# Two one-hots from table products, weight splits one block ahead, and a larger early share of gather steps in a PEER encoder kernel

## The chip, the core and the metric

The kernel runs on one core of a Trainium2 chip. The metric is the time of one execution on the device, in microseconds (us). The core has a matrix engine (TensorE, PE in the rows, with its weight loads as PEld), a vector engine (VectorE, DVE), a scalar engine (ScalarE, ACT), GpSimd (POOL) and a sync engine (SyncE, SP). Each engine runs its own instructions strictly in the order in which they stand in its queue. Sixteen DMA engines move data between the device's memory, where all inputs and the kernel's DRAM buffers lie, and the on-chip memory (SBUF). TensorE writes into PSUM.

## The reference

One encoder layer on 1024 tokens of width 1024. The change lies in its last part, the PEER feed-forward: each token picks, for each of 8 heads, 16 of 16384 experts; an expert number is e = 128 i + j.

```python
def chunk(xc):
    q = (xc @ w_q).reshape(C, PEER_HEADS, 2, PEER_DK // 2)
    s = jnp.einsum('chpd,hpnd->chpn', q, sub_keys, preferred_element_type=jnp.float32)
    sv, si = lax.top_k(s, PEER_TOPK)
    ...
    best, pos = lax.top_k(cand, PEER_TOPK)
    eidx = jnp.take_along_axis(cidx, pos, axis=-1)
    g = jax.nn.softmax(best, axis=-1)
    u = u_tab[eidx]
    a = jax.nn.gelu(jnp.einsum('chkd,cd->chk', u, xc, ...), approximate=False)
    vv = v_tab[eidx]
    return jnp.einsum('chk,chkd->cd', (g * a).astype(vv.dtype), vv)
```

## The kernel before

The 1024 tokens are 8 tiles of 128. Tiles 0 to 2 are **gathered**: for each of a token's 128 chosen experts one indirect DMA on GpSimd brings that expert's row of 1024 values for each of the tile's 128 tokens (tile `grow`, 128x1024, six buffers), first rows of the u table, which VectorE multiplies with the token (L1249), then rows of the v table, which it adds to `gacc` (L1257). One such row load with its use is called a gather use here; there are 3 x 256 = 768. Tiles 3 to 7 (640 tokens) are **dense**: all 16384 experts are computed for them, as 128 blocks of 128 experts.

A dense **u block** (`u_part`) loads 512 KB of transposed weights into `ur` (one buffer), splits them into a high and a low part (`uh` by a ScalarE copy, L291; `ul` by a VectorE subtraction, L292; two buffers each), does 2 x 8 x 3 matmuls of 320 columns (L285 to L287, three for each product of split numbers) into PSUM, and a GELU into `A`. Blocks 1 to 72 (EARLY) run in the early stage, use the four PSUM buffers `ps_x`, and store `A` to DRAM (`a_d`); the other 56 run in the late stage. I number the blocks by the order of their `ul` on VectorE: "split 10" is the L292 of the tenth.

The late stage weighs each block's `A` with a dense gate matrix G (L1359) and multiplies the result with the v table (`vr`, `vh`, `vl`; 128 blocks in two halves of 512 columns, 15 matmuls each).

G is built in the early stage. `route` finds the chosen experts of a tile on VectorE (some 180 instructions a tile). For a dense tile it writes j, and j*j in two parts, to DRAM (`jx_d`) and reads it back as `jl`, and transposes i and the gates into `ig`. `build_g` then goes through the tile in 32 **hot steps** of four tokens: the one-hot of i (`p1`) is an is_equal on VectorE (L1160); the one-hot of j times the gate (`p2`) comes from a product of `jl` with the table `par_r` (L1153, "parabola": 2*j*j' - j*j - j'*j' + 1, which is 1 where j = j' and not positive elsewhere) and a Relu on ScalarE (L1166); four matmuls of `p2` and `p1` give four tokens' G (L1182), ScalarE copies them out (L1183), and every eighth step 2 MB go to `g_d`.

The order is not written out by hand. The program order is set by generators: before each early block so much of `weights()` (routing and hot steps) as its planned cost asks for, after it so many gather steps as `tick` pays for. EHEAD is the share of the gather steps that the early stage is planned to do. A scheduler then orders each engine's queue by its own estimate of times; a buffer of a pool is handed on in program order.

Of the kernel before, what the change touches and what calls it, by code (L numbers as in the profile page):

```python
# [282 lines left out]
def mm3(nc, out, L, R, start, stop):  # L283

    nc.tensor.matmul(out, L[0], R[0], start=start, stop=False)  # L285
    nc.tensor.matmul(out, L[0], R[1], start=False, stop=False)  # L286
    nc.tensor.matmul(out, L[1], R[0], start=False, stop=stop)  # L287


def split(nc, hi, lo, src):  # L290
    nc.scalar.copy(hi, src)  # L291
    return nc.vector.tensor_sub(lo, src, hi)  # L292
# [3 lines left out]
def layer(ctx: ExitStack, tc: tile.TileContext, a: dict, out: bass.AP):  # L296
    nc = tc.nc
# [9 lines left out]
    dram = ctx.enter_context(tc.tile_pool(name="dram", bufs=1, space=DRAM))  # L307
    ident = const.tile([P, P], F32, name="ident")
# [237 lines left out]
    with tc.tile_pool(name="rqp", bufs=1, side="right") as rqp:  # L546
# [4 lines left out]
        for cts, ones in (((0, 1), ones_q), ((2,), ones_kv)):  # L551
# [6 lines left out]
            r = rqp.tile([P, T], F32, name="r")  # L558
# [7 lines left out]
    for j in (*range(4, 12), *range(4)):  # L566
# [166 lines left out]
    with tc.tile_pool(name="ltp", bufs=2, side="right") as ltp:  # L733
# [70 lines left out]
        for c in range(2):  # L804
            cs = slice(256 * c, 256 * c + 256)
# [119 lines left out]
    iota = keep.tile([P, P], F32, name="iota")  # L925
# [89 lines left out]
    def route(tt, rp, done):  # L1015
# [69 lines left out]
        ij = rp.tile([P, 2, P], I32, name="r_ij")
        nc.vector.tensor_scalar(ij[:, 0], ei, 7, None, op0=ALU.arith_shift_right)
        nc.vector.tensor_scalar(ij[:, 1], ei, 127, None, op0=ALU.bitwise_and)
        ijf = rp.tile([P, P], F32, name="r_ijf")
        nc.vector.tensor_copy(ijf, ij[:, 0])
        jj = rp.tile([P, P], I32, name="r_jj")  # L1090
        nc.vector.tensor_tensor(jj, ij[:, 1], ij[:, 1], op=ALU.mult)
        jp = rp.tile([P, 2, P], I32, name="r_jp")
        nc.vector.tensor_scalar(jp[:, 1], jj, 127, None, op0=ALU.bitwise_and)
        nc.vector.tensor_scalar(jp[:, 0], jj, 127 << 7, None, op0=ALU.bitwise_and)
        jx = rp.tile([P, 3, P], BF16, name="r_jx")
        nc.vector.tensor_copy(jx[:, 0], ij[:, 1])
        nc.vector.tensor_copy(jx[:, 1:3], jp)
        nc.sync.dma_start(jx_d[tt].rearrange("r t s -> t r s"), jx)
        jl = jls[tt % 2]
        for r in range(3):  # L1100
            nc.sync.dma_start(jl[32 * r:32 * r + 32], jx_d[tt, r].rearrange("(q t) s -> t q s", t=32))
        ps = psO.tile([P, 2, P], F32, name="ps_o0")
        nc.tensor.transpose(ps[:, 0], ijf, ident)
        nc.tensor.transpose(ps[:, 1], w.rearrange("p h k -> p (h k)"), ident)
        ig = rp.tile([P, 2, P], F32, name="ig", bufs=2)
# [28 lines left out]
    CS = 32  # L1134
    GI = 4
    NCS = TD // CS
    jx_d = dram.tile([NT, 3, P, P], BF16, name="jx_d")
    NB = 4
    HOT = 0.69
    g_d = dram.tile([NCS, P, P, CS], F32, name="g_d")  # L1140
# [1 line left out]
    def build_g(ijg, t, gp):  # L1142


        ig, jl = ijg
        steps = [(cs, c4) for cs in range(P // CS) for c4 in range(0, CS, NB)]
        par, hot = {}, {}

        def parabola(n):
            cs, c4 = steps[n]  # L1150
            ps = psO.tile([P, NB, P], F32, name=f"ps_o{n % 2}")
            c = cs * CS + c4
            nc.tensor.matmul(ps, jl[0:98, c // 32], par_r[0:98, c % 32:c % 32 + NB], start=True, stop=True)  # L1153
            par[n] = ps

        def hots(n):
            cs, c4 = steps[n]
            c = cs * CS + c4
            p1 = gp.tile([P, NB, P], F32, name="p1", bufs=4)
            nc.vector.tensor_tensor(p1, iota.unsqueeze(1).to_broadcast([P, NB, P]),  # L1160
                                    ig[:, 0, c:c + NB].unsqueeze(2).to_broadcast([P, NB, P]),
                                    op=ALU.is_equal)
            p2 = gp.tile([P, NB, P], F32, name="p2", bufs=4)
            ps = par.pop(n)
            for j in range(NB):
                nc.scalar.activation(p2[:, j], ps[:, j], AF.Relu, scale=ig[:, 1, c + j:c + j + 1])  # L1166
            hot[n] = p1, p2

        parabola(0)
        parabola(1)  # L1170
        hots(0)
        for n, (cs, c4) in enumerate(steps):
            if n + 2 < len(steps):
                parabola(n + 2)
            if n + 1 < len(steps):
                hots(n + 1)
            if c4 == 0:
                st = gp.tile([P, P, CS], F32, name="gst", bufs=2)
            p1, p2 = hot.pop(n)
            ps = psH.tile([P, NB, P], F32, name="ps_h")  # L1180
            for j in range(NB):
                nc.tensor.matmul(ps[:, j], p2[:, j], p1[:, j], start=True, stop=True)  # L1182
            nc.scalar.copy(st[:, :, c4:c4 + NB], ps.rearrange("p c i -> p i c"))  # L1183
            if c4 + NB == CS:
                nc.sync.dma_start(g_d[t * (P // CS) + cs], st)
            yield HOT


# [103 lines left out]
    with tc.tile_pool(name="rp", bufs=1, side="left") as rp, \  # L1292
# [249 lines left out]
```

## Time and profile before

| | us |
|---|---|
| median of 3 runs (3285.90 to 3292.27) | 3290.01 |
| the profiled execution | 3294.61 |
| its span on the core | 3292.8 |
| the early stage: from split 3 to split 74 | 1077.9 to 1925.1 |
| the late stage, from split 74 to the end of the span | 1925.1 to 3292.8 |

The profiled execution is 1.8 us longer than its span and 4.6 us above the median of the runs. Over the whole span PE is busy 91%, VectorE 83%, ScalarE 38% and GpSimd 32%; PE's granted clock is 0.959 of full speed (2.4 GHz) in the mean. Stages differ, so everything below is read by stage.

### The profile page before, as it was taken

The page shows a single profiled execution, that of the slowest core. Times are in us where ns is not written, and L with a number is a line of the kernel's source. Part 1 is how long each engine was busy: PE and PEld are TensorE (multiplying, and loading weights), DVE is VectorE, ACT ScalarE, POOL GpSimd, SP SyncE. Part 2 cuts the span into 40 slices and gives each one's busy share as a digit, 9 for nine tenths or more (in the row PEclk, how much of TensorE's full clock was granted, in tenths as well). Part 3 has the DMA queues.
Part 4 walks back from the last instruction along what each step waited for, and adds up shares of the span by engine and source line. Part 5 has one row for each costly group of instructions (what it writes and reads, how often), then busy time and mean ns, then how long its engine had stood idle before and what let it go on. Part 6 is the DMA issues. An engine that isn't in the chain of part 4 may idle for free.

```text
span 3292.8 us, 44912 instructions
## 1 busy us (share of the span) xinstructions
PE 3005.8 (91%) x15582; PEld 2558.8 (78%) x15582; DVE 2734.7 (83%) x5514; ACT 1256.6 (38%) x2454; POOL 1052.8 (32%) x797
## 2 busy tenths in 40 slices
PE   6999788889999779999898789998999999899997
PEld 5676566556699679888897778886888888788886
DVE  7556788888757899999998758888888888888877
ACT  4544434455523226756564122222222222222222
POOL 0000000000000351332344726554655555555550
PEclk9999898889999889999999999999999999999999
DMA  5344733412444777877888989999999898999983
GB/s 170 104 147 141 241 106 106 109 55 64 144 154 144 280 262 239 309 273 275 309 297 314 368 299 354 332 348 352 339 341 343 312 343 310 349 329 333 333 307 134
DMA packets 355065, 828.88 MB, mean 252 GB/s; under 512 B 34345, under 2 KB 144851, under 8 KB 351253
## 3 DMA queue, kind: packets, MB, share of 16 engines
q1 hardware_dynamic: 243957, 422.25, 38.2%
q0 software_dynamic: 110592, 402.70, 34.0%
q8 instruction: 123, 2.02, 0.3%
q10 hardware_dynamic: 288, 1.05, 0.1%
q14 instruction: 105, 0.86, 0.1%
HBM read 715.52 MB, written 110.33 MB: 251 GB/s over the span
## 4 chain that ended last, share of the span: by engine, by line
PE 48%; DVE 28%; DMA 12%; issue 6%; ACT 3%; POOL 1%; SPq 1%; DVEq 0%; ACTq 0%; POOLq 0%
PE ps_x L285 8%; PE ps_x L287 8%; PE ps_x L286 8%; DMA vr<-in_peer_v 6%; DVE gacc L1257 4%; DVE grow L1249 3%; PE ps_h L287 3%; PE ps_h L285 3%; PE ps_h L286 3%; PE ps_o L286 2%; PE ps_o L285 2%; PE ps_o L287 2%; DVE ul L292 2%; DVE p L1160 2%; DMA ur<-in_peer_uT 1%
## 5 line engine op out<-in xcount | busy, mean ns | idle before, releaser
L1236 POOL DMA_INDIRECT grow<-in_peer_u,eid x384 | 532.8, 1387 | 590.2 <-DVE grow L1249 204.7
L1236 POOL DMA_INDIRECT grow<-in_peer_v,eid x384 | 506.1, 1318 | 589.7 <-DVE gacc L1257 296.1
L1257 DVE SCALAR_TENSOR_TENSOR gacc<-grow,dot,gacc 128x1024 f32<-128x1024 f32 x381 | 487.2, 1279 | 14.7 <-DMA grow<-in_peer_v,eid 10.1
L1249 DVE SCALAR_TENSOR_TENSOR grow<-grow,gh 128x1024 f32<-128x1024 f32 x384 | 459.6, 1218 | 23.5 <-DMA grow<-in_peer_u,eid 23.0
L287 PE MATMUL ps_x<-hd,ul 128*128 128x320 f32 x1152 | 370.9, 331 | 62.5 <-DVE ul L292 62.3
L285 PE MATMUL ps_x<-hd,uh 128*128 128x320 f32 x1152 | 376.8, 328 | 33.1 <-ACT uh L291 33.1
L286 PE MATMUL ps_x<-hd,uh 128*128 128x320 f32 x1152 | 372.5, 324 | 0.0
L286 PE MATMUL ps_x<-vl,wh 128*128 128x512 f32 x864 | 343.7, 398 | 4.0 <-DVE vl L292 4.0
L287 PE MATMUL ps_x<-vh,wl 128*128 128x512 f32 x864 | 338.6, 395 | 0.0
L285 PE MATMUL ps_x<-vh,wh 128*128 128x512 f32 x864 | 304.6, 400 | 31.9 <-ACT vh L291 22.2
L291 ACT CAST vh<-vr 128x512 fp32r<-128x512 f32 x256 | 155.9, 619 | 449.5 <-DMA vr<-in_peer_v 303.3
L287 PEld LDWEIGHTS ps_x<-hd,ul 128*128 128x128 f32 x1152 | 226.3, 199 | 76.6 <-DVE ul L292 73.2
L285 PE MATMUL ps_h<-hd,uh 128*128 128x320 f32 x896 | 277.7, 310 | 2.6 <-ACT A L1209 2.6
L286 PE MATMUL ps_h<-hd,uh 128*128 128x320 f32 x896 | 277.2, 310 | 0.0
L287 PE MATMUL ps_h<-hd,ul 128*128 128x320 f32 x896 | 275.4, 310 | 0.0
L292 DVE TENSOR_TENSOR vl<-vr,vh 128x512 fp32r<-128x512 f32 x256 | 173.3, 685 | 118.2 <-ACT vh L291 117.3
L285 PEld LDWEIGHTS ps_x<-hd,uh 128*128 128x128 f32 x1152 | 229.3, 199 | 40.0 <-ACT uh L291 39.0
L286 PEld LDWEIGHTS ps_x<-hd,uh 128*128 128x128 f32 x1152 | 228.8, 199 | 0.8
L285 PEld LDWEIGHTS ps_x<-vh,wh 128*128 128x128 f32 x864 | 164.3, 192 | 69.6 <-ACT vh L291 24.4
L291 ACT CAST uh<-ur 128x1024 fp32r<-128x1024 f32 x128 | 134.7, 1052 | 211.1 <-DMA ur<-in_peer_uT 121.3
L292 DVE TENSOR_TENSOR ul<-ur,uh 128x1024 fp32r<-128x1024 f32 x128 | 155.8, 1217 | 60.9 <-ACT uh L291 59.1
L286 PEld LDWEIGHTS ps_x<-vl,wh 128*128 128x128 f32 x864 | 165.8, 192 | 40.9 <-DVE vl L292 7.8
(365 smaller groups left out, 6868.3 us busy)
## 6 DMA issues: line engine op xcount, KB each, us to landing
ur<-in_peer_uT SPq DMA_DIRECT2D x128, 512.0 KB
vr<-in_peer_v SPq DMA_DIRECT2D x256, 256.0 KB
g_d<-gst SPq DMA_DIRECT2D x20, 2048.0 KB
gt<-g_d SPq DMA_DIRECT2D x32, 1280.0 KB
a_d<-A SPq DMA_DIRECT2D x72, 320.0 KB
A<-a_d SPq DMA_DIRECT2D x72, 320.0 KB
fw<-in_dft_fw SPq DMA_DIRECT2D x64, 256.0 KB
wr<-in_w_in SPq DMA_DIRECT2D x16, 512.0 KB
```

The costliest lines, as they stand in the source:

```text
L285: nc.tensor.matmul(out, L[0], R[0], start=start, stop=False)
L286: nc.tensor.matmul(out, L[0], R[1], start=False, stop=False)
L287: nc.tensor.matmul(out, L[1], R[0], start=False, stop=stop)
L291: nc.scalar.copy(hi, src)
L292: return nc.vector.tensor_sub(lo, src, hi)
L1160: nc.vector.tensor_tensor(p1, iota.unsqueeze(1).to_broadcast([P, NB, P]), ig[:, 0, c:c + NB].unsqueeze(2).to_broadcast([P, NB, P]), op=ALU ...
L1236: nc_i = nc.gpsimd.indirect_dma_start(out=t, out_offset=None, in_=a["peer_" + kind], in_offset=bass.IndirectOffsetOnAxis(ap=eid[g][:, k:k ...
L1249: nc.vector.scalar_tensor_tensor(t, t, 1.0, h_t, op0=ALU.mult, op1=ALU.mult, accum_out=d[:, k - k0:k - k0 + 1])
L1257: nc.vector.scalar_tensor_tensor(acc, t, dots[k0][:, k - k0:k - k0 + 1], acc, op0=ALU.mult, op1=ALU.add)
```

## The change

- The one-hot of i is no longer a VectorE comparison. A second table product (into a `ps_x` buffer) and a Relu of 512 columns on ScalarE make it. For this `route` writes i and j and their squares' parts as six rows (`x_d`), `jl` is loaded in six pieces, and only the gates are transposed.
- The first two steps' products of each dense tile are ordered on PE behind the last matmul of the u block written just before them (`issue_after`).
- `u_part` splits the weights of its own block and of the next one before its matmuls.
- EHEAD goes from 0.28 to 0.36.
- The stores of `A` (`a_d`) and of G (`g_d`) are issued from ScalarE's queue and no longer from SyncE's.

```diff
-EHEAD = 0.28
+EHEAD = 0.36
...
-        nc.sync.dma_start(jx_d[tt].rearrange("r t s -> t r s"), jx)
+        xx = rp.tile([P, 3, 2, P], I32, name="r_xx")
+        nc.vector.tensor_scalar(xx[:, 0, 0], ei, 7, None, op0=ALU.arith_shift_right)
+        nc.vector.tensor_scalar(xx[:, 0, 1], ei, 127, None, op0=ALU.bitwise_and)
+        x2 = rp.tile([P, 2, P], I32, name="r_x2")
+        nc.vector.tensor_tensor(x2, xx[:, 0], xx[:, 0], op=ALU.mult)
+        nc.vector.tensor_scalar(xx[:, 1], x2, 127 << 7, None, op0=ALU.bitwise_and)
+        nc.vector.tensor_scalar(xx[:, 2], x2, 127, None, op0=ALU.bitwise_and)
+        xb = rp.tile([P, 6, P], BF16, name="r_xb")
+        nc.vector.tensor_copy(xb, xx.rearrange("p r w s -> p (r w) s"))
+        nc.sync.dma_start(x_d[tt].rearrange("r t s -> t r s"), xb)
...
-            ps = psO.tile([P, NB, P], F32, name=f"ps_o{n % 2}")
             c = cs * CS + c4
-            nc.tensor.matmul(ps, jl[0:98, c // 32], par_r[0:98, c % 32:c % 32 + NB], start=True, stop=True)
-            par[n] = ps
+            par[n] = []
+            for w in range(2):
+                ps = psO.tile([P, NB, P], F32, name=f"ps_o{n % 2}") if w else psX.tile([P, NB, P], F32, name="ps_x")
+                nc.tensor.matmul(ps, jl[0:98, w, c // 32], par_r[0:98, c % 32:c % 32 + NB], start=True, stop=True)
+                par[n].append(ps)
...
-            nc.vector.tensor_tensor(p1, iota.unsqueeze(1).to_broadcast([P, NB, P]),
-                                    ig[:, 0, c:c + NB].unsqueeze(2).to_broadcast([P, NB, P]),
-                                    op=ALU.is_equal)
+            pi, pj = par.pop(n)
+            nc.scalar.activation(p1, pi, AF.Relu)
...
-        parabola(0)
-        parabola(1)
+        with tc.issue_after(ended[-1]) if ended else ExitStack():
+            parabola(0)
+            parabola(1)
...
-                nc.sync.dma_start(g_d[t * (P // CS) + cs], st)
+                nc.scalar.dma_start(g_d[t * (P // CS) + cs], st)
...
+    def u_part(i, psum):
+
+        for n in (i, i + 1):
+            if n < P and n not in ready:
+                u_load(n)
+        uh, ul = ready.pop(i)
...
-            nc.sync.dma_start(a_d[e], A)
+            nc.scalar.dma_start(a_d[e], A)
```

How the queues change, at three places. First PE, before, near block 15, where the transposes of the first dense tile's routing stand (`r_ijf`, `r_w`) and block 15 goes on around them (`ps_x_9939` is its second half; the first products stand behind block 15, inside block 16):

```order
L287 MATMUL ps_x_9939<-hd_7120,ul_9909 128x320
L1103 MATMUL ps_o0_9022<-ident_60,r_ijf_9008 128x128 [waits DVE_49]
L1104 MATMUL ps_o0_9022<-ident_60,r_w_8996 128x128
L285 MATMUL ps_x_9939<-hd_7120,uh_9908 128x320
L286 MATMUL ps_x_9939<-hd_7120,uh_9908 128x320
L287 MATMUL ps_x_9939<-hd_7120,ul_9909 128x320
```

The same place after: the transpose and the first three products of the first dense tile, which need `jl` (loaded after that tile's routing), stand directly behind block 7 (`ul_8873`) and ahead of block 8 (`ps_x_9108`):

```order
L287 MATMUL ps_x_8981<-hd_7120,ul_8873 128x320
L1100 MATMUL ps_o0_9045<-ident_60,r_w_9020 128x128 [waits DVE_49]
L1151 LDWEIGHTS jl1_7577 [waits DMAHW4_49,DMAHW6_49,DMAHW2_49,Pool_49]
L1151 MATMUL ps_x_9049<-par_r_7574,jl1_7577 128x512
L1151 LDWEIGHTS jl1_7577
L1151 MATMUL ps_x_9053<-par_r_7574,jl1_7577 128x512 [waits Activation_49]
L1151 LDWEIGHTS jl1_7577
L1151 MATMUL ps_x_9064<-par_r_7574,jl1_7577 128x512 [waits Activation_49]
L285 MATMUL ps_x_9108<-hd_7120,uh_8950 128x320 [waits Activation_49]
```

Before, blocks 8 to 15 stood ahead of the first product; after, only blocks 1 to 7 do, and block 8 stands behind it. The products take `ps_x` buffers, which the blocks use too.

Second VectorE, before, behind split 44: routing, one-hots of i and gather uses are mixed (the first 12 of the 22 rows up to split 45):

```order
L292 TENSOR_TENSOR ul_13744<-ur_13741,uh_13743 128x1024
L1027 MAX_INDEX r_si_14912<-r_sv_14911,r_s_14909 128x8
L1043 TENSOR_TENSOR r_cand_15412<-r_sv_14911 128x8
L1160 TENSOR_TENSOR p1_13828<-iota_6486,ig_13125 128x512
L1249 SCALAR_TENSOR_TENSOR grow_13804,dot_13809<-grow_13804,gh_8442 128x1024
L1257 SCALAR_TENSOR_TENSOR gacc_8444<-grow_13594,dot_12473,gacc_8444 128x1024
L1026 MAX r_sv_14911<-r_s_14909 128x8
L1249 SCALAR_TENSOR_TENSOR grow_13807,dot_13809<-grow_13807,gh_8442 128x1024
L1160 TENSOR_TENSOR p1_13928<-iota_6486,ig_13125 128x512
L1026 MAX r_sv_14911<-r_s_14909 128x8
L1160 TENSOR_TENSOR p1_13944<-iota_6486,ig_13125 128x512
L1160 TENSOR_TENSOR p1_14005<-iota_6486,ig_13125 128x512
```

VectorE after, from split 44 to split 45 complete: nothing but gather uses (L1266 is the old L1257):

```order
L292 TENSOR_TENSOR ul_13963<-ur_13960,uh_13962 128x1024
L1266 SCALAR_TENSOR_TENSOR gacc_8450<-grow_15564,dot_15038,gacc_8450 128x1024
L1266 SCALAR_TENSOR_TENSOR gacc_8450<-grow_15567,dot_15038,gacc_8450 128x1024
L1266 SCALAR_TENSOR_TENSOR gacc_8450<-grow_15662,dot_15038,gacc_8450 128x1024
L1266 SCALAR_TENSOR_TENSOR gacc_8450<-grow_15667,dot_15038,gacc_8450 128x1024
L1266 SCALAR_TENSOR_TENSOR gacc_8450<-grow_15670,dot_15038,gacc_8450 128x1024
L1266 SCALAR_TENSOR_TENSOR gacc_8450<-grow_15673,dot_15038,gacc_8450 128x1024
L292 TENSOR_TENSOR ul_14065<-ur_14062,uh_14064 128x1024
```

The one-hots are gone from VectorE and gather uses have moved forward into their place: ahead of split 74 stand 256 of the 768 uses before and 381 after.

Counted in VectorE's queue (the number of instructions that stand ahead of a split):

| ahead of | gather uses | routing | splits | one-hots of i |
|---|---|---|---|---|
| split 18, before | 53 | 527 | 17 | 6 |
| split 10, after | 56 | 547 | 9 | 0 |
| split 34, after | 154 | 1125 | 33 | 0 |
| split 74, before | 256 | 1266 | 73 | 160 |
| split 74, after | 381 | 1256 | 73 | 0 |

In the late stage the uses stand about as close as before, 28 to 42 for every 16 of the 256 splits of v weights, up to about the 180th of them; behind that no use is left after the change, where some 130 were left before. In PE's queue after, of the 160 hot steps 5 stand ahead of block 10, 69 between blocks 10 and 34, 86 between 34 and 74.

## Rows read from the trace of the kernel before

**Rows 1.** The page, part 1: busy time, share of the span, instructions.
```profile
PE 3005.8 (91%) x15582; PEld 2558.8 (78%) x15582; DVE 2734.7 (83%) x5514; ACT 1256.6 (38%) x2454; POOL 1052.8 (32%) x797
```

**Rows 2.** Windows: stretch, length, busy PE, PEld, DVE, ACT, POOL, granted clock, DMA share, GB/s.
```profile
1258.00:1500.00 242.00, 229.28 (x1608) 219.25 (x1607) 238.34 (x691) 158.20 (x441) 74.73 (x60) 0.97 0.80 288
1500.00:1754.00 254.00, 236.51 (x1658) 224.69 (x1658) 252.42 (x748) 162.26 (x447) 87.35 (x68) 0.99 0.83 295
1785.00:1890.00 105.00, 77.80 (x440) 73.08 (x438) 81.22 (x99) 16.95 (x30) 74.82 (x54) 0.87 0.95 356
1990.00:2890.00 900.00, 861.76 (x4321) 746.19 (x4320) 783.54 (x1057) 231.00 (x381) 493.09 (x364) 0.98 0.96 339
```

**Rows 3.** Groups of VectorE from 1258 to 1754: busy, mean ns; idle before.
```profile
L1160 DVE TENSOR_TENSOR p<-iota,ig 128x512 f32<-128x512 f32 x150 | 99.2, 677 | 0.9 <-PE ps_h L1182 0.9
L1257 DVE SCALAR_TENSOR_TENSOR gacc<-grow,dot,gacc 128x1024 f32<-128x1024 f32 x65 | 82.7, 1272 | 0.0
L1249 DVE SCALAR_TENSOR_TENSOR grow<-grow,gh 128x1024 f32<-128x1024 f32 x64 | 76.7, 1209 | 0.4 <-DMA grow<-in_peer_u,eid 0.4
```

**Rows 4.** Timeline of VectorE (start, length): splits 18, 58, 73, 74; four one-hots.
```profile
1234.60 2.49 DVE L1160 TENSOR_TENSOR p<-iota,ig 128x512 f32<-128x512 f32 x4
1258.04 1.23 DVE L292 TENSOR_TENSOR ul<-ur,uh 128x1024 fp32r<-128x1024 f32 x1
1754.26 1.23 DVE L292 TENSOR_TENSOR ul<-ur,uh 128x1024 fp32r<-128x1024 f32 x1 [0.39 <-ACT uh L291]
1919.05 1.23 DVE L292 TENSOR_TENSOR ul<-ur,uh 128x1024 fp32r<-128x1024 f32 x1 [4.62 <-ACT uh L291]
1925.13 1.23 DVE L292 TENSOR_TENSOR ul<-ur,uh 128x1024 fp32r<-128x1024 f32 x1 [4.86 <-ACT uh L291]
```

**Rows 5.** Timeline of VectorE in the dense stretch: two splits, gather uses between.
```profile
1859.97 1.22 DVE L292 TENSOR_TENSOR ul<-ur,uh 128x1024 fp32r<-128x1024 f32 x1
1861.11 1.22 DVE L1249 SCALAR_TENSOR_TENSOR grow<-grow,gh 128x1024 f32<-128x1024 f32 x1
...
1867.47 1.22 DVE L1249 SCALAR_TENSOR_TENSOR grow<-grow,gh 128x1024 f32<-128x1024 f32 x1 [1.79 <-DMA grow<-in_peer_u,eid]
...
1872.07 1.22 DVE L292 TENSOR_TENSOR ul<-ur,uh 128x1024 fp32r<-128x1024 f32 x1
```

**Rows 6.** Timeline of ScalarE and PE: block 7's last GELU; the first two table products.
```profile
1145.79 0.44 ACT L1209 ACTIVATE A<-ps_x 128x320 f32<-128x320 f32 x1 [1.46 <-PE ps_x L287]
...
1244.10 0.61 PE L1153 MATMUL ps_o<-par_r,jl 98*128 98x512 bf16 x2
```

**Rows 7.** Timeline of PE: neighbouring matmuls of 320 and 512 columns; four one-hot matmuls.
```profile
2403.37 0.31 PE L285 MATMUL ps_h<-hd,uh 128*128 128x320 f32 x1
2403.52 0.31 PE L286 MATMUL ps_h<-hd,uh 128*128 128x320 f32 x1
...
2406.53 0.39 PE L285 MATMUL ps_x<-vh,wh 128*128 128x512 f32 x1
2406.76 0.39 PE L286 MATMUL ps_x<-vl,wh 128*128 128x512 f32 x1
...
1257.44 1.05 PE L1182 MATMUL ps_h<-p,p 128*128 128x128 f32 x8
```

**Rows 8.** DMA issues from 1785 to 1890: count, KB each (512 KB an indirect one).
```profile
ur<-in_peer_uT SPq DMA_DIRECT2D x9, 512.0 KB
grow<-in_peer_u,eid POOLq DMA_INDIRECT x27
grow<-in_peer_v,eid POOLq DMA_INDIRECT x27
```

**Rows 9.** Timeline of ScalarE: one hot step's four Relus, and its copy out.
```profile
1257.20 1.14 ACT L1166 ACTIVATE p<-ps_o,ig 128x128 f32<-128x128 f32 x4 [0.24 <-PE ps_o L1153]
1258.53 0.59 ACT L1183 COPY gst<-ps_h 128x512 f32<-128x512 f32 x1 [0.19 <-PE ps_h L1182]
```

**Rows 10.** Timeline of VectorE in the late stage: the 94th block is weighed.
```profile
2887.59 0.82 DVE L1359 TENSOR_TENSOR A<-A,gt 128x640 f32<-128x640 f32 x1 [3.40 <-DMA gt<-g_d]
```

More of the change, by code (lines that the diff above doesn't have):

```diff
@@ L286, in mm3 @@
     nc.tensor.matmul(out, L[0], R[1], start=False, stop=False)
-    nc.tensor.matmul(out, L[1], R[0], start=False, stop=stop)
+    return nc.tensor.matmul(out, L[1], R[0], start=False, stop=stop)
 def split(nc, hi, lo, src):
@@ L1084, in route @@
         nc.vector.tensor_copy(ei, ef2)
[L1085 to L1097, printed above, removed]
-        nc.sync.dma_start(jx_d[tt].rearrange("r t s -> t r s"), jx)
-        jl = jls[tt % 2]
-        for r in range(3):
-            nc.sync.dma_start(jl[32 * r:32 * r + 32], jx_d[tt, r].rearrange("(q t) s -> t q s", t=32))
@@ L1102, in route @@
[L1102 to L1105, printed above, removed]
+        xx = rp.tile([P, 3, 2, P], I32, name="r_xx")
+        nc.vector.tensor_scalar(xx[:, 0, 0], ei, 7, None, op0=ALU.arith_shift_right)
+        nc.vector.tensor_scalar(xx[:, 0, 1], ei, 127, None, op0=ALU.bitwise_and)
+        x2 = rp.tile([P, 2, P], I32, name="r_x2")
@@ new lines, in route @@
+        nc.vector.tensor_tensor(x2, xx[:, 0], xx[:, 0], op=ALU.mult)
[4 more added lines that the diff above has]
+        nc.sync.dma_start(x_d[tt].rearrange("r t s -> t r s"), xb)
+        jl = jls[tt % 2]
+        for r in range(6):
+            nc.sync.dma_start(jl[32 * (r // 2):32 * (r // 2) + 32, r % 2],
+                              x_d[tt, r].rearrange("(q t) s -> t q s", t=32))
@@ L1106, in route @@
+        ps = psO.tile([P, P], F32, name="ps_o0")
+        nc.tensor.transpose(ps, w.rearrange("p h k -> p (h k)"), ident)
+        ig = rp.tile([P, P], F32, name="ig", bufs=2)
         nc.scalar.copy(ig, ps)
@@ L1136, in layer @@
     NCS = TD // CS
-    jx_d = dram.tile([NT, 3, P, P], BF16, name="jx_d")
+    x_d = dram.tile([NT, 6, P, P], BF16, name="x_d")
     NB = 4
@@ L1159, in hots @@
             p1 = gp.tile([P, NB, P], F32, name="p1", bufs=4)
-            nc.vector.tensor_tensor(p1, iota.unsqueeze(1).to_broadcast([P, NB, P]),
-                                    ig[:, 0, c:c + NB].unsqueeze(2).to_broadcast([P, NB, P]),
-                                    op=ALU.is_equal)
             p2 = gp.tile([P, NB, P], F32, name="p2", bufs=4)
-            ps = par.pop(n)
+            pi, pj = par.pop(n)
+            nc.scalar.activation(p1, pi, AF.Relu)
             for j in range(NB):
-                nc.scalar.activation(p2[:, j], ps[:, j], AF.Relu, scale=ig[:, 1, c + j:c + j + 1])
+                nc.scalar.activation(p2[:, j], pj[:, j], AF.Relu, scale=ig[:, c + j:c + j + 1])
             hot[n] = p1, p2
-        parabola(0)
-        parabola(1)
+        with tc.issue_after(ended[-1]) if ended else ExitStack():
+            parabola(0)
+            parabola(1)
         hots(0)
@@ L1194, in layer, with u_load @@
     loads = []
-    def u_part(i, psum):
+    ready, ended = {}, []
+    def u_load(i):
         ur = up.tile([P, ND, P], F32, name="ur", bufs=1)
@@ L1201, in u_part @@
         split(nc, uh, ul, ur)
+        ready[i] = uh, ul
+    def u_part(i, psum):
[3 more added lines that the diff above has]
+        uh, ul = ready.pop(i)
         A = up.tile([P, TD], F32, name="A", bufs=3)
@@ L1206, in u_part @@
             for ct in range(ND):
-                mm3(nc, ps, (uh[:, ct], ul[:, ct]), (hd[:, 0, ct, s], hd[:, 1, ct, s]),
-                    ct == 0, ct == ND - 1)
+                r = mm3(nc, ps, (uh[:, ct], ul[:, ct]), (hd[:, 0, ct, s], hd[:, 1, ct, s]),
+                        ct == 0, ct == ND - 1)
             nc.scalar.activation(A[:, s], ps, AF.Gelu)
+        ended.append(r.ins)
         return A
@@ L1300, in layer @@
                              own.unsqueeze(2).to_broadcast([98, 32, P]))
-        jls = [gp.tile([98, 4, P], BF16, name=f"jl{i}") for i in range(2)]
+        jls = [gp.tile([98, 2, 4, P], BF16, name=f"jl{i}") for i in range(2)]
         for jl in jls:
```

## The prediction, made before the changed kernel had run

> **What bounds the kernel now.** I read the page's busy shares first [rows 1], then windows by stage [rows 2], then VectorE's groups and timeline in the early stage [rows 3 to 5]. No engine is busy all the time over the whole span, so the bound has to be found stage by stage. From 1258 to 1754 us VectorE is busy 238.3 of 242 and 252.4 of 254 us, while PE is at 229 and 237 and the DMA share at 0.80 and 0.83 [rows 2]: VectorE is the bound there. From 1785 to 1890 nothing is left on VectorE but splits and gather uses; it drops to 81 of 105 us, PE to 78 at a granted clock of 0.87, and the DMA engines rise to a share of 0.95 at 356 GB/s [rows 2]. Between two splits there VectorE stands still for gather rows that have not landed (1.79 us before one) [rows 5], and a block takes 12.1 us from split 1859.97 to split 1872.07 [rows 5]; where no use lies between two splits it takes 6.1 us (1919.05 to 1925.13) [rows 4]. So with some six gather uses in each block the DMA engines are the bound. In the late stage PE is busy 862 of 900 us at clock 0.98, with DMA at 0.96 [rows 2]: PE leads, with little room on the DMA side.
>
> **Unit prices.** On VectorE, start to start: a split 1.14 us (1859.97 to 1861.11) [rows 5]; a one-hot of i (2.49 - 0.08)/4 = 0.60 us [rows 4]; a gather use 1.18 us, that is 1.209 and 1.272 us in the mean less the 0.08 by which neighbours overlap, plus a little waiting [rows 3, 5]. Routing: 490.8 busy us from split 18 to split 58 [rows 2, 4], less 129 uses, 40 splits and 150 one-hots (152 + 46 + 90), leaves 203 us for 727 routing instructions, 0.28 us each. On PE: a matmul of 320 columns 0.147 us (0.15 between two starts), so a u block of 48 takes 7.05; one of 512 columns 0.23; the four matmuls of a hot step 0.86 as an estimate from 1.05 us for the group with its last one's drain [rows 7]. A hot step is then 0.86 + 0.23 = 1.09 us before and 1.32 after, since it gets a second table product.
>
> **The change, step by step, against the profiled 3294.6 us.**
>
> *First blocks.* In the queue after, the first table products stand behind block 7; they need `jl`, which VectorE's routing of the first dense tile has to finish. Block 7 ended at 1145.8, the products ran at 1244.1 [rows 6]. PE, which did blocks 8 to 15 in that time, now waits for about 95 us. Ahead of split 10 stands after what stood ahead of split 18 before: 3 more uses, 20 more routing instructions, 8 fewer splits, 6 fewer one-hots, 3.5 + 5.6 - 9.1 - 3.6 = -4 us. Split 18 was at 1258.0 [rows 4], so split 10 comes at **1254**, eight blocks behind.
>
> *Splits 10 to 34.* VectorE: 98 uses, 24 splits, 578 routing instructions: 116 + 27 + 162 = 305 us. PE: 24 blocks and 69 hot steps, 169 + 91 = 260. DMA: 51 MB of rows, 20 MB of `ur` and `a_d`, 18 MB of G and 4 MB of routing input, 93 MB, at 356 GB/s 261. VectorE bounds: split 34 at **1559**.
>
> *Splits 34 to 74.* VectorE: 227 uses, 40 splits, 131 routing instructions: 268 + 46 + 37 = 351 us. PE: 40 blocks and 86 hot steps: 282 + 114 = 396. DMA: 227 x 0.524 = 119 MB of rows, 40 x 0.852 = 34 MB of `ur` and `a_d`, 86/8 stores of 2.1 MB = 22.5, about 1 of routing input: 176.5 MB. At the 356 GB/s of the dense stretch (54 gather loads and 9 to 10 blocks in 105 us [rows 2, 8]) that is 496 us; at that rate over its share of 0.95, 375 GB/s, 471. This is the dense stretch's pattern, 5.7 uses a block, made four times as long. The uses stand ahead of the splits in VectorE's queue, so blocks can't run past them. Split 74 comes at 1559 + 496 = **2055**, where it was at 1925.1 [rows 4]: +130.
>
> *Late stage.* 387 uses are left instead of 512, but up to about the 180th split of v weights they stand as close as before; there I take no gain. The rest began before near the 94th weighing, at 2887.6 [rows 10], and took 405 us to the span's end, for PE work of 13 u blocks and 1200 matmuls of 512 columns: 92 + 272 = 364 us at 0.227 each [rows 7]. At most 41 us can be won, part of that is the tail behind the last matmul; I take 18, with 0 and 41 for the range.
>
> *Costs put at nothing.* The second Relu is 0.6 us a step by the copy of the same size, a step is then 1.14 + 0.59 + 0.60 = 2.33 us of ScalarE [rows 9], 373 us for 160 in a stage of 800; its price if not hidden is a rival. The stores' issues go to an engine busy 38% [rows 1]. Splitting a block ahead gains nothing that I can see: `ur` has one buffer still, and the blocks wait for VectorE's uses, not for the order of splits. SP loses the waits for `A`, but keeps `ur` loads behind `x_d` and its six loads, behind VectorE again; bound 0 to 5 us a tile, within the range.
>
> Sum: 3294.6 + 130 - 18 = 3406.6 for a profiled execution; less the 4.6 by which that lay above the median, **3402**, which I round to 3400.
>
> **Rivals.**
>
> *A, the DMA engines carry more.* If they kept 420 GB/s, splits 34 to 74 would take 420 us, and from 446 GB/s on PE's 396; split 74 at 1955 to 1979, +30 to +54, time 3302 to 3326. For: single slices of the dense stretch go above its mean. Against: the share was 0.95 at 356 GB/s over 105 us, and 0.96 at 339 over 900 [rows 2]. The Trainium skill (DMA: Bandwidth & Descriptors, Bandwidth) gives 425 GB/s for one transfer of 16 MB with the pair's other core idle, which would put this case at A's lower end. The rows here stay well below that, so A gets 0.17.
>
> *B, faster.* The gathers that have left the late stage free PE there at once, not only behind the last use. From 1925.1 to the end are 1368 us for 56 u blocks and 3840 matmuls of 512 columns, 395 + 872 = 1267; with some 20 us of tail that can't go, 80 can be won. With A's +30 that is 3294.6 + 30 - 80 - 4.6 = 3240; it decides once split 74 comes before 1925 + 80 = 2005. For: VectorE and the DMA engines have 125 uses less to do there. Against: the uses keep their density up to the 180th split. 0.09.
>
> *C, ScalarE sets the pace of the hot steps.* Steps stand in clusters, 2.33 us on ScalarE against 1.32 on PE; with the difference in full, 1.01 us x 69 = 70 us in splits 10 to 34, where PE has 305 - 260 = 45 to spare, and 87 in 34 to 74, where it has 100. +25, or +60 if the spare time is spent badly: 3425 to 3460. 0.16.
>
> *D, it cancels.* Half of A and half of B meet near zero, or the new order does in effect what the old one did: 3283 to 3297. 0.05.
>
> **How the numbers follow.** The forecast (3370 to 3425) has 0.53. The range 3310 to 3460 takes in the forecast, C and the larger part of A, about 0.83. A measurement of this kernel can tell about 0.2% from no change, 6.6 us. Slower is forecast, C and nearly all of A: 0.85; the same is D and a little of A: 0.06; faster is B: 0.09.
>
> **What would show it.** Right: PE idle for some 95 us behind block 7 with VectorE full; split 10 near 1254, split 34 near 1560, split 74 between 2030 and 2080; a DMA share of 0.93 or more and VectorE below 0.8 from split 34 on; a PE clock below 0.9 there; a late stage 0 to 41 us shorter than 1368. Wrong: split 74 before 2005, or a DMA rate above 400 GB/s over the second stretch (A, B); ScalarE the releaser of most PE waits (C).

## The result: 4.4% slower, and the profile after

| | before | after | predicted |
|---|---|---|---|
| median, us | 3288.27 | 3433.31 (3426.81 to 3436.56) | 3400 (3310 to 3460) |
| ratio to before, 95% interval | | 1.0437 (1.0416 to 1.0459) | 1.034 |
| the profiled execution, us | 3294.61 | 3430.11 | 3406.6 |
| split 10 | 1168.0 | 1248.4 | 1254 |
| split 34 | 1453.6 | 1568.9 | 1559 |
| split 74 | 1925.1 | 2079.9 | 2055 |
| split 74 to the span's end | 1367.7 | 1348.4 | 1350 |

The three splits in VectorE's timeline after (start, length; [rows 4] has split 74 of before):

```profile
1248.42 1.21 DVE L292 TENSOR_TENSOR ul<-ur,uh 128x1024 fp32r<-128x1024 f32 x1
1568.87 1.22 DVE L292 TENSOR_TENSOR ul<-ur,uh 128x1024 fp32r<-128x1024 f32 x1 [0.27 <-ACT uh L291]
2079.89 1.23 DVE L292 TENSOR_TENSOR ul<-ur,uh 128x1024 fp32r<-128x1024 f32 x1 [0.41 <-ACT uh L291]
```

The page's busy shares after; before they were [rows 1]. VectorE gave up 83 us, while PE and ScalarE took on 38 and 80:

```profile
PE 3043.8 (89%) x15737; PEld 2575.5 (75%) x15737; DVE 2652.1 (77%) x5344; ACT 1336.3 (39%) x2616; POOL 1033.2 (30%) x797
```

Windows of the kernel after, with the columns of [rows 2] (stretch, length, busy PE, PEld, DVE, ACT, POOL, granted clock, DMA share, GB/s):

```profile
1148.00:1248.00 100.00, 15.39 (x91) 13.79 (x92) 100.00 (x354) 12.86 (x31) 40.15 (x33) 0.55 0.62 193
1248.00:1410.00 162.00, 148.90 (x989) 136.47 (x987) 161.00 (x546) 102.23 (x271) 61.56 (x49) 0.95 0.82 293
1410.00:1569.00 159.00, 141.19 (x921) 128.02 (x921) 147.53 (x475) 94.74 (x243) 64.42 (x51) 0.96 0.85 304
1569.00:1670.00 101.00, 88.36 (x575) 81.15 (x576) 86.57 (x170) 60.21 (x153) 60.64 (x42) 0.92 0.90 330
1670.00:1770.00 100.00, 86.96 (x550) 78.12 (x549) 64.29 (x120) 57.50 (x153) 59.06 (x46) 0.93 0.94 358
1770.00:1870.00 100.00, 88.69 (x592) 81.16 (x592) 75.65 (x115) 64.60 (x159) 48.77 (x33) 0.93 0.88 319
1870.00:1970.00 100.00, 89.22 (x585) 81.10 (x583) 65.64 (x72) 59.33 (x157) 59.54 (x48) 0.95 0.96 368
1970.00:2080.00 110.00, 85.39 (x481) 79.62 (x481) 85.72 (x104) 19.91 (x33) 76.97 (x60) 0.89 0.98 371
1569.00:2080.00 511.00, 438.62 (x2779) 401.15 (x2779) 377.86 (x577) 261.56 (x651) 304.97 (x227) 0.92 0.93 349
2145.00:2700.00 555.00, 533.88 (x2692) 461.47 (x2691) 487.15 (x656) 146.98 (x241) 310.75 (x225) 0.99 0.95 338
...
3000.00:3428.00 428.00, 409.76 (x2057) 355.78 (x2055) 213.90 (x300) 116.00 (x188) 17.66 (x14) 0.98 0.44 139
```

The line 1569 to 2080 is the whole stage from split 34 to split 74, the five lines above it are its parts. Read from the top: PE does 15 us of work in 100 while VectorE is full; up to 1569 VectorE leads; from there to 2080 the DMA share is 0.88 to 0.98 and VectorE falls to 64 to 86 of 100; in the late stage PE is at 0.96 again; from 3000 on the gather is over (DMA 0.44), and PE is no busier than before that.

PE's wait in its timeline (start, length, in brackets the idle time before and its releaser, that is what ended it):

```profile
1151.11 0.47 PE L1100 MATMUL ps_o<-ident,r_w 128*128 128x128 f32 x1 [15.92 <-DVE r_w L1082]
1233.08 1.44 PE L1151 MATMUL ps_x<-par_r,jl 98*128 98x512 bf16 x3 [81.50 <-DMA jl<-x_d]
1233.96 0.83 PE L285 MATMUL ps_x<-hd,uh 128*128 128x320 f32 x1
1234.58 0.47 PE L286 MATMUL ps_x<-hd,uh 128*128 128x320 f32 x1
1234.85 0.47 PE L287 MATMUL ps_x<-hd,ul 128*128 128x320 f32 x1
...
1237.42 0.31 PE L285 MATMUL ps_x<-hd,uh 128*128 128x320 f32 x1
1237.57 0.31 PE L286 MATMUL ps_x<-hd,uh 128*128 128x320 f32 x1
```

15.92 + 81.50 = 97 us pass with one transpose, until `jl` has landed; then block 8 starts. The first three products run straight ahead of it, in the blocks' own `ps_x` buffers.

### The profile page after: what moved, and what is told of

Read it like the earlier page. It is cut to its first block, busy times and chain, and to the rows that moved or that the text cites. A ratio compares the mean times of both kernels' runs of the same rounds, so it can differ in the third digit from the quotient of the medians.

```text
span 3428.3 us, 45099 instructions
## 1 busy us (share of the span) xinstructions
PE 3043.8 (89%) x15737; PEld 2575.5 (75%) x15737; DVE 2652.1 (77%) x5344; ACT 1336.3 (39%) x2616; POOL 1033.2 (30%) x797
## 4 chain that ended last, share of the span: by engine, by line
PE 38%; DVE 13%; DMA 9%; issue 6%; POOL 2%; ACT 2%; SPq 0%; DVEq 0%; ACTq 0%; POOLq 0%
PE ps_x L285 7%; PE ps_x L287 6%; PE ps_x L286 6%; PE ps_h L286 3%; PE ps_h L287 3%; PE ps_h L285 3%; DMA grow<-in_peer_u,eid 2%; DVE grow L1258 2%; POOL grow L1245 2%; PE ps_o L286 2%; DMA vr<-in_peer_v 2%; PE ps_o L285 2%; PE ps_o L287 2%; DVE gacc L1266 2%; DMA grow<-in_peer_v,eid 2%
## 5 line engine op out<-in xcount | busy, mean ns | idle before, releaser
L1245 POOL DMA_INDIRECT grow<-in_peer_u,eid x384 | 514.5, 1340 | 492.9 <-issue 145.0
L1266 DVE SCALAR_TENSOR_TENSOR gacc<-grow,dot,gacc 128x1024 f32<-128x1024 f32 x381 | 487.1, 1279 | 35.5 <-DMA grow<-in_peer_v,eid 29.2
L285 PE MATMUL ps_x<-vh,wh 128*128 128x512 f32 x864 | 312.2, 395 | 24.2 <-ACT vh L291 19.1
```

The costliest lines, as they stand in the source:

```text
L1245: nc_i = nc.gpsimd.indirect_dma_start(out=t, out_offset=None, in_=a["peer_" + kind], in_offset=bass.IndirectOffsetOnAxis(ap=eid[g][:, k:k ...
L1266: nc.vector.scalar_tensor_tensor(acc, t, dots[k0][:, k - k0:k - k0 + 1], acc, op0=ALU.mult, op1=ALU.add)
```

## The experiments

My theory has two causes. (1) The first products stand behind block 7 because they take the `ps_x` buffers, which the blocks use too, so PE waits for routing and the blocks fall eight splits behind. (2) The 125 gather uses moved ahead of split 74 make the DMA engines the bound of splits 34 to 74. The rivals: one of the two alone; ScalarE's pace (case C); the split a block ahead; the stores on another queue. Every kernel was timed beside the kernel before on its chip, and ratios are to that.

### Four kernels that take the two causes apart

`e1_ehead28` is the changed kernel with one constant undone:

```diff
-EHEAD = 0.36
+EHEAD = 0.28
```

> The changed kernel with EHEAD back at 0.28 and nothing else undone. In its queues the first table products still stand behind block 7, so PE's early wait stays; ahead of split 74 stand 256 gather uses as before the change (146 ahead of split 34, 240 ahead of split 50, 256 from split 58 on). My theory has two causes: (1) the early wait, which puts the blocks eight splits behind, and (2) the 125 moved uses, which make the DMA engines the bound of splits 34 to 74. By it: split 10 at 1248, split 34 near 1560; splits 34 to 50 bounded by DMA as now, 74 MB at 349 GB/s = 212 us; splits 50 to 74 at PE's pace, 24 x 7.05 + 43 x 1.32 = 226 us; split 74 near 2000, late stage back at 1368: 3368 median (3350 to 3385), some 65 us faster than the changed kernel and 80 slower than before. If the moved uses were the whole cause: 3290 to 3310. If the early wait were the whole cause (or ScalarE's pace, which this edit leaves as it is): 3425 to 3440.

`e2_pso` keeps the products out of the blocks' buffers:

```diff
-                ps = psO.tile([P, NB, P], F32, name=f"ps_o{n % 2}") if w else psX.tile([P, NB, P], F32, name="ps_x")
+                ps = psO.tile([P, NB, P], F32, name=f"ps_o{w}")
...
-        with tc.issue_after(ended[-1]) if ended else ExitStack():
-            parabola(0)
-            parabola(1)
+        parabola(0)
...
-            if n + 2 < len(steps):
-                parabola(n + 2)
             if n + 1 < len(steps):
+                parabola(n + 1)
```

> The changed kernel with both table products of a step in the ps_o buffers (that of i in ps_o0, that of j in ps_o1, one step ahead in place of two) and without the ordering behind blocks: nothing of them is in the blocks' ps_x buffers any more. EHEAD stays 0.36. In PE's queue the first product then stands behind block 16 as before the change, so PE's early wait should be gone; ahead of split 74 stand 350 uses (53 ahead of split 18). My theory: split 18 near 1258 as before the change; splits 18 to 74 bounded by DMA, 297 x 0.524 + 56 x 0.852 + 20 x 2.1 + some 8 = 254 MB at 349 GB/s = 727 us; split 74 near 1985, late stage 1368 less some 15: 3335 median (3310 to 3360). If the early wait costs nothing in the end (DMA bounds everything): 3415 to 3440. If ScalarE's pace of the hot steps is the cause: 3425 or more, since one step of lead in place of two makes it worse.

`e3_pso28` has both edits:

> Both edits together: both table products in the ps_o buffers, no ordering behind blocks, and EHEAD 0.28. No early wait (first product behind block 17), 256 uses ahead of split 74 as before the change. What is left of the change is the one-hot of i from ScalarE, the split a block ahead and the stores on ScalarE's queue. My theory (two causes, both gone): from split 18 at 1258, VectorE has 205 uses, 56 splits and 741 routing instructions, 242 + 64 + 207 = 513 us, PE 56 blocks and 160 hot steps, 395 + 211 = 606 us, so PE bounds and split 74 comes between 1865 and 1925; late stage 1368: 3230 to 3290 median, likeliest 3260, faster than both kernels. If the one-hot on ScalarE sets the pace (one step of lead, 2.33 us of ScalarE a step): 3300 or more.

`e4_noissue` drops the ordering alone:

```diff
-        with tc.issue_after(ended[-1]) if ended else ExitStack():
-            parabola(0)
-            parabola(1)
+        parabola(0)
+        parabola(1)
```

> The changed kernel without the ordering of the first products behind the block ahead of them; the product of i stays in the ps_x buffers. In PE's queue the first product stands behind block 7 all the same, since the ps_x buffers are handed on in program order. My theory (the place comes from the shared buffers and not from the ordering): no change, 3433 within 15. If the ordering makes the early wait: as without that wait, 3335 to 3380.

Measured (median, ratio with its 95% interval, and the splits in the profiled execution):

| | median | ratio | split 10 | split 34 | split 74 | from there to the end |
|---|---|---|---|---|---|---|
| after: wait, 381 uses ahead | 3433.3 | 1.0437 (1.0416 to 1.0459) | 1248.4 | 1568.9 | 2079.9 | 1348 |
| e1: wait, 256 uses | 3346.8 | 1.0158 (1.0123 to 1.0194) | 1252.9 | 1558.9 | 2000.1 | 1345 |
| e2: no wait, 350 uses | 3383.7 | 1.0289 (1.0262 to 1.0316) | 1158.9 | 1484.2 | 2023.1 | 1357 |
| e3: no wait, 256 uses | 3297.4 | 1.0022 (1.0006 to 1.0038) | 1163.6 | 1457.9 | 1938.0 | 1353 |
| e4: as after, no ordering | 3436.9 | 1.0446 (1.0418 to 1.0473) | 1251.3 | 1576.1 | 2087.8 | 1348 |

The stretch of the wait, in e1 and in e3 (windows, columns as above):

```profile
1148.00:1248.00 100.00, 9.73 (x43) 8.32 (x44) 100.00 (x366) 8.49 (x18) 40.87 (x32) 0.52 0.60 188
```

```profile
1148.00:1248.00 100.00, 79.88 (x477) 77.29 (x477) 100.00 (x341) 21.87 (x35) 47.64 (x30) 0.90 0.76 250
```

In e1 PE waits as in the changed kernel; in e3 it works 80 of 100 us beside a VectorE that is just as full. The two causes add up. Taking the uses back is worth 87 us with the wait (after against e1, 125 uses), and taking the wait away after that is worth 49 (e1 against e3, 256 uses in both). Together that is 136 of the 145 us. The other way round the steps are 50 (after against e2) and 86 (e2 against e3), but they aren't as clean: e2 has 31 uses fewer ahead of split 74 than the changed kernel, at 0.7 us each some 22 of its 50 us, and its 86 us are for 94 uses, 0.9 us each. How much the wait alone costs with all 381 uses moved is therefore not shown. e3, without either, is 0.2% from the kernel before. Neither cause alone explains the result: if the uses were all of it, e1 should have come below 3310, if the wait were, above 3425; it came at 3347. e4 shows that `issue_after` is not what puts the products behind block 7: nothing changes without it. e2 also takes one step of lead in place of two; but the kernel before has two steps of lead, in `ps_o`, and no such wait, so the shared buffers are what is left.

My sizes were off, though. e1's split 74 came where I had put it (2000), but its late stage took 1345 us and not 1368. e2 and e3 were 49 and 37 us slower than my likeliest values: splits 34 to 58 took 360 and 365 us in both, where PE's own sum is 24 x 7.05 + 89 to 101 x 1.32 = 287 to 302. No engine is full there over the whole stretch; I come back to it.

### Is it the bytes of the moved rows?

`e5_halfrow` loads half rows and keeps VectorE's work (the rest of the edit, not shown, lets VectorE read each half row twice):

```diff
-            t = gap.tile([P, D], F32, name="grow", bufs=GB)
+            t = gap.tile([P, D // 2], F32, name="grow", bufs=GB)
...
-                out=t, out_offset=None, in_=a["peer_" + kind],
+                out=t, out_offset=None, in_=a["peer_" + kind].rearrange("e (h d) -> (e h) d", h=2),
```

> The changed kernel with gather rows of 512 values in place of 1024 (256 KB a load in place of 512); VectorE still works on 1024 values a use, reading each half row twice. The output is not the layer's, since half of each expert row is left out. What counts is the stage from split 34 to split 74, which takes 511 us in the changed kernel; 216 uses lie in it here, 227 there. If the DMA engines bound it (the prediction's step): 115 MB in place of 178, 323 us at 356 GB/s, so PE's 396 us take over: 400 to 430 us, DMA share below 0.85, granted clock near 0.98. If VectorE's uses or ScalarE's hot steps bound it, the work there is the same: 490 to 515 us. The early wait of PE behind block 7 stays in either case.

Splits 34 to 74 took 443 us in place of 511 (one execution). Three windows of that stage:

```profile
1569.00:1670.00 101.00, 97.58 (x675) 91.23 (x674) 90.57 (x142) 69.19 (x185) 64.32 (x48) 0.98 0.80 268
1670.00:1770.00 100.00, 96.27 (x662) 87.85 (x661) 87.00 (x167) 73.07 (x190) 57.23 (x45) 1.00 0.79 268
1770.00:1870.00 100.00, 90.16 (x603) 82.69 (x603) 76.73 (x89) 58.79 (x152) 57.35 (x51) 0.98 0.83 281
```

PE goes from 87 to 89 of 100 up to 90 to 97, its clock to 0.98 or more, and VectorE does more work per microsecond than with whole rows. So the bytes bound the stage: with nearly the same uses for VectorE and the same steps for ScalarE it is 68 us shorter. It is 13 us above the top of what I expected: the transfer is the larger part of the bound, not all of it. (Eleven uses fewer lie in the stage, 13 us of VectorE's time, so a little of the 68 is theirs.) A half row also comes round faster through the six `grow` buffers; whether the engines' rate or the time that one row takes is the limit, e5 doesn't separate. More buffers with whole rows were not run.

### ScalarE, the split ahead, the stores

`e6_relu2` doubles the new Relu:

```diff
             nc.scalar.activation(p1, pi, AF.Relu)
+            nc.scalar.activation(p1, pi, AF.Relu)
```

> The changed kernel with the Relu that makes the one-hot of i done twice, with the same result: 160 x 0.6 = 96 us more work for ScalarE in the early stage, and each hot step 2.9 us long there. If ScalarE sets the pace of the hot steps (the prediction's case C): 40 to 97 us slower than the changed kernel, 3475 to 3530. If it is hidden beside the DMA bound, as the forecast put it at nothing: 3433 within 15.

Measured 3471.8, ratio 1.0539 (1.0492 to 1.0585): 38 us slower than the changed kernel for 96 us more of ScalarE's work. That lies between the two expectations. Of ScalarE's groups from 1569 to 2080 us the new Relu is L1160, and in e6 L1161 repeats it (line, operation, count, busy, mean ns, idle before). First the changed kernel, then e6:

```profile
L1162 ACT ACTIVATE p<-ps_o,ig 128x128 f32<-128x128 f32 x336 | 99.5, 432 | 0.2
L1180 ACT COPY gst<-ps_h 128x512 f32<-128x512 f32 x88 | 55.3, 635 | 13.8 <-PE ps_h L1179 10.9 <-PE ps_o L1151 1.0 <-PE ps_x L287 0.7
L1160 ACT ACTIVATE p<-ps_x 128x512 f32<-128x512 f32 x86 | 53.3, 656 | 11.3 <-PE ps_x L1151 11.1
```

```profile
L1161 ACT ACTIVATE p<-ps_x 128x512 f32<-128x512 f32 x88 | 59.9, 700 | 0.3
...
L1160 ACT ACTIVATE p<-ps_x 128x512 f32<-128x512 f32 x88 | 55.7, 659 | 8.1 <-PE ps_x L1151 8.1
```

Split 74 came 25 us later (2104.8). Nine more uses stand ahead of it in e6; at the 0.7 us that a moved use costs (87 us for 125) they make some 6 of the 25. The late stage, where no Relu was added, took 14 us longer, which is within what the order of instructions moves there (1339 to 1377 us over the kernels with whole rows). That leaves 19 to 32 us for the 96. So a Relu of 0.66 us in a hot step is hidden for the larger part, not wholly: case C is wrong as the main cause, and the price of nothing is wrong too.

`e7_noahead` splits only a block's own weights:

```diff
-        for n in (i, i + 1):
+        for n in (i,):
```

> The changed kernel with the weights split for the block's own use only, not a block ahead. The prediction put the split ahead at nothing, since the blocks wait for VectorE's uses and for rows: 3433 within 15. If the split ahead itself costs (two u blocks' weights wanted at once, earlier ur loads beside the gathers): 20 or more faster; if it helps: 20 or more slower.

`e8_sync` puts the stores back:

```diff
-                nc.scalar.dma_start(g_d[t * (P // CS) + cs], st)
+                nc.sync.dma_start(g_d[t * (P // CS) + cs], st)
...
-            nc.scalar.dma_start(a_d[e], A)
+            nc.sync.dma_start(a_d[e], A)
```

> The changed kernel with the stores of A and of G issued from SyncE's queue again. The prediction gave this part 0 to 5 us a tile: 3433 within 20. If the stores on ScalarE's queue hold up its Relus and copies (a wait for its own work ahead of each issue): 20 to 60 faster. If they relieve the ur loads: 5 to 25 slower.

e7: 3405.4, ratio 1.0350 (1.0313 to 1.0387), 28 us faster than the changed kernel; splits 10 to 34 take 302 us in place of 320, with 7 uses fewer there (8 us), and the late stage takes 1339. e8: 3446.1, ratio 1.0469 (1.0434 to 1.0503), whose interval overlaps that of the changed kernel, with 6 more uses ahead of split 74.

### Parts alone, on the kernel before, and the best mix

`e9_best` is e3 with the edit of e7. `e10_act_only`, `e11_ahead_only` and `e12_ehead_only` are the kernel before with one part of the change: the stores on ScalarE's queue, the split a block ahead (the diff below), EHEAD 0.36.

```diff
-    def u_part(i, psum):
+    ready = {}
+    def u_load(i):
...
+        ready[i] = uh, ul
+    def u_part(i, psum):
+        for n in (i, i + 1):
+            if n < P and n not in ready:
+                u_load(n)
+        uh, ul = ready.pop(i)
```

> The changed kernel with what the runs so far found costly undone: both table products in the ps_o buffers (no ordering behind blocks), EHEAD 0.28, weights split for the block's own use. What is left of the change is the one-hot of i from ScalarE and the stores on ScalarE's queue. Without the split's undoing this was 3297 (0.2% slower than before). If what the split ahead costs is there without the early wait too (28 us in the changed kernel): 3270, 0.6% faster than before (3255 to 3285). If it costs only where VectorE holds the blocks up behind the early wait: 3285 to 3300, no change from before.

> The kernel before with one part of the change alone: the stores of A and of G are issued from ScalarE's queue. Its order is otherwise nearly that of before (256 uses ahead of split 74 in both). If taking the stores off SyncE frees the ur loads, as the 13 us of the run with the stores put back suggests: 3275 to 3285, 0.2 to 0.4% faster than before. If those 13 us were only the six more uses that stood in the early stage there: 3290 within 5.

> The kernel before with one part of the change alone: u_part splits the weights a block ahead. 256 uses ahead of split 74 as before. If the split ahead costs by itself: 3300 to 3320. If it only costs where VectorE holds the blocks up (the changed kernel between splits 10 and 34): 3290 within 7.

> The kernel before with one part of the change alone: EHEAD 0.36 in place of 0.28. In its queues only 292 uses stand ahead of split 74 (256 before, 381 in the changed kernel), since VectorE is full with one-hots and routing up to about split 58. If each use moved ahead of split 74 costs there what it costs the changed kernel (125 uses, 87 us, 0.7 us each): 36 uses, +25 us, 3315 to 3322. If the early stage has room for them beside VectorE's other work, or the late stage gives back what they cost: 3297 within 8. If EHEAD's value in itself costs 87 us: 3380.

| | median | ratio | split 34 | split 74 | from there to the end |
|---|---|---|---|---|---|
| e9: e3 without the split ahead | 3302.3 | 1.0019 (1.0008 to 1.0029) | 1455.1 | 1940.1 | 1359 |
| e10: before, stores on ScalarE's queue | 3301.2 | 1.0012 (0.9996 to 1.0028) | 1460.6 | 1925.8 | 1377 |
| e11: before, split a block ahead | 3265.0 | 0.9915 (0.9897 to 0.9932) | 1438.3 | 1908.2 | 1351 |
| e12: before, EHEAD 0.36 (292 uses ahead of split 74) | 3317.5 | 1.0068 (1.0048 to 1.0089) | 1491.0 | 1971.4 | 1348 |

e9 missed the 3270 that I held likeliest and came out as its second case, no change from before: the split ahead costs nothing once the early wait is gone (3297 with it, 3302 without, on another chip; the ratios are 1.0022 and 1.0019). e10: the stores' queue moves nothing that can be measured. e12 hit its first case: 36 moved uses cost 22 us by the ratio, 0.6 us each, about as much as each of the 125 of the changed kernel. Its dense stretch is the pattern of [rows 2], now longer:

```profile
1770.00:1870.00 100.00, 80.81 (x458) 76.63 (x457) 81.91 (x102) 19.76 (x36) 72.36 (x51) 0.86 0.97 364
1870.00:1970.00 100.00, 81.57 (x456) 76.45 (x454) 77.98 (x87) 19.61 (x33) 66.65 (x53) 0.88 0.98 364
```

**e11 beats both kernels**, by 0.85%, against all that I expected of it. Its 33 us lie in three places: 7 ahead of split 3 (1070.6 against 1077.9; but e7 and e9, which split nothing ahead, have 1072 too), 10 from there to split 74, 16 in the late stage. Waits of PE for `ul` from split 3 to 1925 fell from 62 to 49 us, which covers the middle piece only. The same edit is worth +28 us in the changed kernel, nothing in e3 and -33 on the kernel before. It changes the place of many instructions in the scheduler's order, and which of them make the difference I can't say: that stays open.

## Why the prediction was right, and where it was not

**The first blocks: right.** The wait was put at some 95 us and is 97; split 10 was put at 1254 and came at 1248.4. Its cause, the products ahead of block 8 in PE's queue, holds (e1, e3), and e2 and e4 add that the shared buffers set the place.

**Splits 10 to 34: right in what bounds, 15 us short.** VectorE's sum was 305 us; it was busy 161 of 162 and 147.5 of 159 us, 308.5 together, so the sum is good to 1% and the other 12 us are idle, which the sum had left out. e7 has 302 us here, 8 of the difference from seven uses fewer. Some 10 us may so be the split ahead, costed at nothing; why it costs here and not in e3 is open.

**Splits 34 to 74: right in what bounds, 15 us short.** The bytes were 178.5 MB (176.5 put), but the rate was 349 GB/s in the mean and not 356. The stage alternates. Three stretches of the changed kernel:

```profile
1620.00:1650.00 30.00, 24.66 (x154) 23.07 (x155) 30.00 (x39) 13.67 (x36) 17.85 (x10) 0.84 0.68 215
1672.00:1697.00 25.00, 24.95 (x174) 22.85 (x173) 13.20 (x21) 17.33 (x50) 15.16 (x13) 1.00 1.02 412
1995.00:2080.00 85.00, 65.88 (x369) 61.54 (x367) 65.87 (x75) 15.46 (x26) 59.85 (x47) 0.88 0.98 361
```

From 1620 to 1650 VectorE is full, with routing among the uses, row buffers come free late, and the transfers fall to 215 GB/s; from 1672 to 1697 the transfers lead and VectorE is at half. Dividing all bytes by one rate, or all work by one engine, gave too short a time for this stage: in each stretch another engine leads, and the one that was summed stands idle for a part. Here the miss was 3%; in my expectations of e2 and e3, where I took the longest engine's sum, it was the larger part of 49 and 37 us.

**Case A** asked for 420 GB/s over the whole stage. The 412 over 25 us shows that the engines can nearly do that; the stage doesn't let them. The Trainium skill (DMA: Bandwidth & Descriptors, Bandwidth) gives 425 GB/s for a lone large transfer, to which the 412 come close; the same page (Where 436 GB/s comes from) names about 358 as what binds transfers from device memory, which those 25 us exceed. The measurement decides: neither is the rate of this stage.

**The late stage: the number right by luck (-19, put at -18), its reason wrong.** I took the gain from the 125 uses that had left its end. But e1 has all 512 uses left and takes 1345 us there, e12 with 476 takes 1348, and the changed kernel with 387 takes 1348; with 512 left the others take 1351 to 1377. The time doesn't follow the number of uses that are left. The end of e1 (DMA 0.84, gather still running) and of the changed kernel (0.44, the last line of its windows above) have nearly the same PE; first e1's windows:

```profile
2145.00:2700.00 555.00, 544.73 (x2764) 474.67 (x2763) 491.21 (x664) 147.51 (x244) 298.01 (x228) 0.99 0.97 343
...
3000.00:3345.00 345.00, 323.23 (x1618) 278.75 (x1616) 292.07 (x402) 89.91 (x149) 153.38 (x114) 0.98 0.84 295
```

PE is busy 0.94 of the last 345 us in e1, and 0.96 of the last 428 after. So taking uses from the end brought nothing, and case B, which wanted 80 us back, was wrong for this change. The 19 us are within what small edits of the order move there.

That is not to say that the rows cost the late stage nothing while they are loaded, which I overlooked. e5, with some 450 uses left that bring half the bytes, took 1317 us there (one execution), 31 less than the changed kernel and less than any kernel with whole rows. Here is one stretch of it in the changed kernel, then in e5 (windows, columns as above):

```profile
2700.00:3000.00 300.00, 291.01 (x1492) 254.78 (x1491) 263.87 (x355) 78.09 (x128) 159.26 (x123) 0.99 0.97 344
```

```profile
2700.00:3000.00 300.00, 298.30 (x1547) 262.75 (x1546) 276.80 (x369) 86.13 (x142) 154.09 (x118) 1.00 0.77 239
```

The change left the uses as dense as before up to 3057 us, so it could not win these microseconds.

**Costs put at nothing.** The Relu: not nothing, by e6 0.2 to 0.3 us for each microsecond added. The split ahead: not nothing, with either sign. The stores: nothing (e10), as put. **Case C** as the main cause is out: e1 and e3 keep every ScalarE step and are 87 and 136 us faster. PE's waits from 1569 to 2080 need a second look (in us, times, longest):

```profile
PE ps_x L285 <- ACT uh L291: 30.3, 20, 3.4
PE ps_o L1151 <- ACT p L1162: 19.4, 20, 4.1
PE ps_x L287 <- DVE ul L292: 15.0, 11, 5.7
```

With the smaller lines they add up to 72 us, and ScalarE is the releaser of 56. So the sign that I had named for case C, ScalarE the releaser of most PE waits, did come. But only 21 us of them are for the Relus and 34 for `uh`, the high half of the weights, and these two follow the transfers: in e5, with the Relus as they were, the waits of PE from split 34 to split 74 are 22 us, 5 for the Relus and 3 for `uh`. VectorE in turn waits 60 us for rows in the changed kernel's stage:

```profile
DVE grow L1258 <- DMA grow<-in_peer_u,eid: 38.2, 27, 4.9
DVE gacc L1266 <- DMA grow<-in_peer_v,eid: 21.6, 14, 6.2
```

**The other signs.** From split 34 on VectorE is at 0.74 (below 0.8, as put) and the DMA share at 0.93 in the mean, but 0.90 and 0.88 in two of the five windows; split 74 lies just inside its bounds (2079.9 of 2080). PE's granted clock was to be below 0.9 and is 0.92, with PE busy 0.86 of the stage; of the five windows only the last has less (0.89, with PE busy 0.78).

The terms put the profiled execution at 3406.6; it was 3430.1. The 23.5 us are -5.6 (split 10), +15.4, +15.0 and -1.3 (late stage).

## What to carry to other kernels

Before work is moved from one stage to another, ask of both stages which engine ends last: 125 gather steps cost 0.7 us each where the DMA engines bound, and taken from the end of the stage where PE led they gave back nothing, although the DMA share there was 0.96. A new user of a buffer pool that is handed on in program order takes a place in the queue of the old users: the first products in the blocks' `ps_x` buffers held PE for 97 us, which cost 49 in the end (e1 against e3). Freeing an engine brought nothing by itself here, where others were nearly full too: e9, which keeps only the one-hot of i off VectorE (some 96 us) and the stores on ScalarE's queue, is 0.2% slower than before. PE was busy 0.93 to 0.95 of that stretch already [rows 2] and got a second product in each hot step; that this is what took the gain is likely, but no run isolates it.

## What the runs showed that I had not expected

- The time hardly depends on the planned share itself but on the order that results: EHEAD 0.36 moves 125 uses in the changed kernel (381 against 256) and 36 in the kernel before (292 against 256), since there VectorE's one-hots and routing keep them back.
- The DMA engines reach 412 GB/s over 25 us with rows, stores and weights mixed, and 361 at a share of 0.98 over 85 us: a share near 1 doesn't tell the rate.
- The granted clock fell to 0.55 over the stretch of PE's wait. Behind it the block's first matmuls of 320 columns start 0.27 us apart (1234.58 and 1234.85), where [rows 7] have 0.15: 1.2 GHz against 2.4. By 1237.42 they are back at 0.15, so this costs 1 to 2 us beside a wait of 97.
